# A two-layer decoder trunk on one core: other first loads, a first step by k tiles, and the first three blocks of each layer in turn by pairs of k tiles

## The chip, the cores and the metric

The kernel runs on one core of one Trainium2 chip. The metric is the device time of one execution in microseconds, as the median of three runs. Engines are called by the names of the profile: PE is TensorE, DVE VectorE, ACT ScalarE, POOL GpSimd and SP SyncE (which here only issues transfers).

## What is computed

The reference is a decoder trunk of two layers, for one sequence of 256 tokens with 2048 channels, all in float32:

```python
proj = rms_norm(x, norm_g) @ w_in        # 2048 -> D_IN columns, cut into segments
mixed = [fox(q, k, v, f), diff(q, k, v), moba(q, k, v), gla(q, k, v, a)]   # each 512 wide
gated = concat([group * silu(gate) for group, gate in zip(mixed, gates)])
x = x + gated @ w_out                    # 2048 -> 2048
```

and, after the second layer, one more RMS norm. This is the reference in outline: FoX is attention with a forget gate, diff the difference of two softmax maps, MoBA attention over chosen blocks of keys, and GLA a linear attention whose gate comes from a narrow projection `gla_a` (16 columns) through a matrix `gla_wa2` and a log-sigmoid.

## The kernel before

**Products.** A float32 product is made of three products of rounded parts: each weight `raw` is split into `hi` (a rounded copy, made by ACT, `hi_of`, line 425) and `lo = raw - hi` (DVE, `lo_of`, line 428). The left side, the normalised and transposed input, lies in SBUF as `hTp` with a high and a low half for each of its 16 k tiles of 128 channels. PE then multiplies high by hi, low by hi, and high by lo (`multiply`, line 1169; the matmul itself is issued by a helper on line 276).

**Steps.** The weights stream through in steps (`_steps`, line 133). A block is a range of up to 512 output columns, and a step is two k tiles of a block. A step costs one transfer into `raw` (four buffers), one hi, one lo (four buffers each) and 12 matmuls: 3 products, 2 k tiles, 2 halves of 128 tokens. `prepare(i)` makes hi and lo of step i and issues the load of step i + 4; it is called three steps ahead of `multiply`. All these loads go through SP's queue, in the order of the program.

**The first three blocks of a layer.** Block 0 has 348 columns (`gla_a` and a part of a gate), block 1 has 512 (GLA's q and k), block 2 has 348 (a gate's rest, FoX's forget gate, a part of FoX's v). Their 24 steps are interleaved, by the sort key on line 140: before, two steps of block 0, two of block 1, two of block 2, and so on. Blocks 0 and 1 accumulate in the PSUM pool `mm` (two buffers), block 2 in a `side` buffer. All other blocks follow one by one. Steps are counted from 0, so that step 24 is the first behind the three blocks.

**The start.** PE first runs `WARM` matmuls on zeros (line 368). The first loads are: x^T, in chunks of four k tiles (`load_x`, line 1086; the first chunk in two halves), the norm's weights `ngt`, the first step's weights in two halves (the first half on ACT's queue, the second on SP's), the next three steps' weights, and a table of constants `ct` on ACT's queue (line 1234). x^T is scaled and split into `hTp` by `split_xt`, k tiles 0 and 1 on DVE, the others' high half on ACT.

**What hangs on the first blocks.** Once the last step of a block is multiplied, `settle` evicts it. From block 0 comes `an` (the 16 gate columns), which PE transposes with `ct`'s identity; DVE copies it to `at`; PE makes `al` from `at` and `wa`; ACT and DVE make its log-sigmoid (`two`, with two loads of a function table) and DVE its running sum. From block 1 come GLA's q and k (`four`): DVE transposes them in squares, SP writes them to DRAM in four transfers `far<-four` (line 310), POOL reads them back turned (`four<-far`, line 312), and ACT puts them in order (`four<-four`, 128x1024). From block 2 come `fx`, FoX's forget gate, with a log-sigmoid of its own (`fe`), and `ct,fh` and `ct,fl` products of FoX's chain. All GLA pieces meet in the factors `eight` and `tq` and in the product `side<-tq,eight` on PE, which stands behind step 40 in layer 0 and behind step 184 in layer 1. These pieces are background tasks, written as generators: `tick` (line 257) runs some of their pieces after each step, into the same in-order queues in which hi, lo, loads and matmuls stand. So what the program writes first, an engine does first.

**At the layer's end** `residual` adds the out-projection to `xs` on DVE (`xs<-mm,xs`) and so frees an `mm` buffer for the next layer's blocks.

Of the kernel before, what the change touches and what calls it, by code (L numbers as in the profile page):

```python
# [21 lines left out]
P = 128  # L22
SEQ = 256
# [10 lines left out]
NEG = -1.0e30  # L34
RAW_BUFS = 4
PART_BUFS = 4
WARM = 10
X_AT = (24, 28, 32, 36)
T4 = 10
T2 = 6  # L40
# [88 lines left out]
LAYER = 20  # L129
FIRST = tuple(l * LAYER + i for l in range(DEPTH) for i in range(3))  # L130


def _steps():


    steps = []
    for i, b in enumerate(_BLOCKS):
        per = b["per"]
        for j in range(0, KT, per):
            key = (i // LAYER * LAYER, j // 4, i) if i in FIRST else (i, 0, i)  # L140
            if b["w"] == "w_out" and b["cols"][0][0] < 1024:
                key = (i - b["cols"][0][0] // 512, max(j // 4, 1), i)
            steps.append((key, len(steps), {"block": i, "kts": b["kts"][j:j + per], "first": j == 0, "last": j + per == KT}))
    steps = [s for _, _, s in sorted(steps, key=lambda z: z[:2])]
    at = 0
    for s in steps:
        s["at"] = at
        at += P * len(s["kts"]) * _BLOCKS[s["block"]]["n"]
    return steps


def in_steps(w_in, w_out):

    w, flat = {"w_in": w_in, "w_out": w_out}, []
    for s in _steps():
        b = _BLOCKS[s["block"]]
        for_kt = [np.concatenate([w[b["w"]][b["l"], k * P:(k + 1) * P, c:c + n] for c, n in b["cols"]], 1) for k in s["kts"]]
        flat.append(np.stack(for_kt, 1).reshape(-1))
    return np.concatenate(flat)
# [48 lines left out]
def hybrid_trunk(  # L208
# [17 lines left out]
    nc = tc.nc  # L226
# [14 lines left out]
    s4 = Slots(wk, "four", T4)  # L241
# [32 lines left out]
    def matmul(out, lhsT, rhs, start, stop, tiles=1):  # L274
        left["pe"] += int(np.prod(rhs.shape[1:])) * (4 if lhsT.dtype == F32 else 1) / 2400.0 / tiles
        t_.matmul(out, lhsT, rhs, start=start, stop=stop)  # L276
# [57 lines left out]
    ct = cp.tile([P, CONST["f"].shape[1]], F32, name="ct")  # L334
    ngt = cp.tile([P, DEPTH, KT], F32, name="ngt")
# [29 lines left out]
    def keep_warm(n):  # L365
        warm = side.get([P, 1024])
        for _ in range(n):
            t_.matmul(warm[:, :512], zeros[:, :P], zeros, start=True, stop=True)
        side.put(warm)

    keep_warm(WARM)
    nc.scalar.activation(halfpow, halfpow, AF.Copy)
# [52 lines left out]
    def hi_of(hi, src, scale=1.0):  # L425
        a_.activation(hi, src, AF.Copy, scale=scale)

    def lo_of(lo, src, hi):
        v_.tensor_sub(lo, src, hi.bitcast(F32))
# [649 lines left out]
    plan = []  # L1079
    for z in _steps():  # L1080
        b = blocks[z["block"]]
        plan.append({**z, "block": b, "need": {(b["need"], b["l"], k // 4) for k in z["kts"]}})

    xts = []

    def load_x(chunk):
        xts.append(s4.get([P, 4, SEQ]))
        if chunk == 0:
            nc.sync.dma_start(ngt, norm_gt)
        for part in (slice(0, 2), slice(2, 4)) if chunk == 0 else (slice(0, 4),):  # L1090
            nc.sync.dma_start(xts[chunk][:, part], xt[:, chunk * 4 + part.start:chunk * 4 + part.stop])

    def load(i):
        s = plan[i]
        if i < 24 and i % 6 == 0:
            load_x(i // 6)
        per, n = s["block"]["per"], s["block"]["n"]
        raw = wst.tile([P, STEP_W], F32, name="raw", bufs=RAW_BUFS)
        raw = raw[:, :per * n]
        s["raw"] = raw.rearrange("p (j c) -> p j c", j=per)  # L1100
        src = weights[s["at"]:s["at"] + P * per * n].rearrange("(p c) -> p c", p=P)
        if i == 0:
            nc.scalar.dma_start(raw[:, :n], src[:, :n])
            nc.sync.dma_start(raw[:, n:], src[:, n:])
        else:
            nc.sync.dma_start(raw, src)

    def xt_hi(kt):
        src, g = xts[kt // 4][:, kt % 4], ngt[:, 0, kt:kt + 1]
        if kt < 2:  # L1110
            v_.tensor_scalar(hT[0][:, kt], src, g, None, op0=OP.mult)
        else:
            hi_of(hT[0][:, kt], src, g)

    def xt_lo(kt):
        v_.scalar_tensor_tensor(hT[1][:, kt], xts[kt // 4][:, kt % 4], ngt[:, 0, kt:kt + 1], hT[0][:, kt].bitcast(F32),
                                op0=OP.mult, op1=OP.subtract)

    def split_xt(kts):

        for kt in kts:
            xt_hi(kt)
        for kt in kts:
            xt_lo(kt)
        if kts[-1] % 4 == 3:
            ready.add(("h", 0, kts[-1] // 4))
# [29 lines left out]
    def parts_of(s):  # L1156
        per, n = s["block"]["per"], s["block"]["n"]
        for name in ("hi", "lo"):
            if s["block"]["kind"] == "apart":
                s[name] = s4.get([P, per, n], F32R)  # L1160
                continue
            t = wst.tile([P, PART_W], F32R, name=name, bufs=PART_BUFS)
            s[name] = t[:, :per * n].rearrange("p (j c) -> p j c", j=per)
        if s is plan[0] or s is plan[1]:
            split_xt(s["kts"])
        hi_of(s["hi"], s["raw"])
        lo_of(s["lo"], s["raw"], s["hi"])

    def multiply(s):
        b = s["block"]  # L1170
        n, (lh, ll) = b["n"], b["lhs"]
        if s["first"]:
            b["ps"] = side.get([P, 1024]) if b["aside"] else mm.tile([P, 1024], F32, name="mm")
        ps = b["ps"]
        if b["kind"] == "apart":
            b.setdefault("steps", []).append(s)
            if s["last"]:
                b["ps1"] = side.get([P, 1024])
            for m, o, steps in ((0, ps[:, :n], [s]), (1, b.get("ps1"), b["steps"])):
                if m == 1 and not s["last"]:  # L1180
                    break
                for z in steps:
                    for j, kt in enumerate(z["kts"]):
                        first, last = z["first"] and j == 0, z["last"] and j == len(z["kts"]) - 1
                        hi, lo, ts = z["hi"][:, j], z["lo"][:, j], slice(m * P, (m + 1) * P)
                        matmul(o[:, :n], lh[:, kt, ts], hi, first, False)
                        matmul(o[:, :n], lh[:, kt, ts], lo, False, False)
                        matmul(o[:, :n], ll[:, kt, ts], hi, False, last)
            return
        order = list(enumerate(s["kts"]))  # L1190
        end = s["last"], len(order) - 1
        for x, part in ((lh, "hi"), (ll, "hi"), (lh, "lo")):
            for j, kt in order:
                for m in range(2):
                    matmul(ps[:, m * 512:m * 512 + n], x[:, kt, m * P:(m + 1) * P], s[part][:, j],
                           s["first"] and j == 0 and x is lh and part == "hi", part == "lo" and (True, j) == end)
# [12 lines left out]
    ahead = PART_BUFS - 1  # L1209

    def prepare(i):
        if 0 < i < 24 and i % 6 == 0:
            split_xt([i // 6 * 4 + k for k in range(4)])
        if i < len(plan):
            parts_of(plan[i])
        if i + RAW_BUFS < len(plan):
            load(i + RAW_BUFS)
# [13 lines left out]

    for i in range(RAW_BUFS):
        load(i)
    nc.scalar.dma_start(ct, const)
    for i in range(ahead):
        prepare(i)
    s4.put(zeros)
    g_.memset(tq, 0.0)
    tasks += [constants()]
# [2 lines left out]
    for i, s in enumerate(plan):  # L1242
        if ("r", 0) not in ready:
            next(rms, None)
        prepare(i + ahead)
        if i in X_AT:
            c = slice(X_AT.index(i) * 512, X_AT.index(i) * 512 + 512)
            nc.sync.dma_start(xs[:, :, c], x[0, :, c].rearrange("(m p) c -> p m c", p=P))
        settle(waiting, s["first"] and len(waiting) > 1)
        while not s["need"] <= ready:  # L1250
            tick(False)
        multiply(s)
        if s["last"] and s["block"]["done"]:
            waiting.append(s["block"])
        give_time()
        tick()
    while tasks:
        tick(False)
    b = plan[-1]["block"]
# [31 lines left out]
```

## Time and profile before

| | us |
|---|---|
| median of three runs (lowest, highest) | 919.61 (918.66, 920.67) |
| the profiled execution | 920.54 |
| its span in the trace | 918.8 |
| PE busy in it | 901.3 |
| DVE busy | 571.5 |
| ACT busy | 524.6 |
| first real matmul | 7.70 |
| GLA's product in layer 0, layer 1 | 111.43, 560.76 |

All times in the profile are from the start of the span, and 1.7 us of the execution lie outside it. A row of the timeline gives start, length, engine, line, operation and tiles, the number of instructions run together, and in brackets how long the engine stood idle before it and what released it. Lines are those of the kernel; L178 is where a helper records all operations of DVE and ACT, so those are told apart by their tiles. PE's matmuls are pipelined, and its busy time includes the time at a lower granted clock.

### The profile page before, as it was taken

What the parts mean: (1) busy time and instruction counts of PE and PEld (TensorE: products, weight loads), DVE (VectorE), ACT (ScalarE), POOL (GpSimd) and SP (SyncE); (2) the same over time, 40 slices, a digit from 0 to 9 for tenths busy, and PEclk for the clock granted to TensorE, in tenths of its full rate; (3) what the DMA queues carried; (4) which work ended last, traced back from release to release, by engine and by line L of the source; (5) the groups of instructions that cost most, each with busy time, mean ns of one, the idle gap of its engine ahead of it and who ended that gap; (6) DMA issues with size and microseconds to landing.
All of it is one profiled execution on the core that took longest, in us unless ns stands there. A gap on an engine that the chain in (4) does not pass through costs nothing.

```text
span 918.8 us, 12421 instructions
## 1 busy us (share of the span) xinstructions
PE 901.3 (98%) x4490; PEld 766.8 (83%) x4490; DVE 571.5 (62%) x831; ACT 524.6 (57%) x819; POOL 38.6 (4%) x55
## 2 busy tenths in 40 slices
PE   8999999999999999999999999999999999999996
PEld 6988789888888888888899887988888888878886
DVE  6765887566558556555655568856655674565662
ACT  6588654664455556535565784566444654754441
POOL 0000000000000010000000000010000000110000
PEclk9999999999999999999999999999999999999998
DMA  8767656587656947757776466667877687587652
GB/s 264 255 206 263 234 182 240 167 301 263 233 183 205 319 156 236 276 200 259 235 231 212 145 235 194 192 212 213 290 231 228 172 264 274 159 307 254 193 164 92
DMA packets 77455, 205.34 MB, mean 223 GB/s; under 512 B 9265, under 2 KB 29137, under 8 KB 77394
## 3 DMA queue, kind: packets, MB, share of 16 engines
q1 hardware_dynamic: 70496, 183.44, 60.7%
q0 software_dynamic: 5408, 19.40, 6.1%
q10 hardware_dynamic: 1490, 1.71, 0.6%
q8 instruction: 35, 0.57, 0.2%
q14 instruction: 26, 0.21, 0.1%
HBM read 184.07 MB, written 20.45 MB: 223 GB/s over the span
## 4 chain that ended last, share of the span: by engine, by line
PE 86%; DMA 4%; ACT 3%; DVE 2%; issue 2%; SPq 1%; DVEq 0%; POOLq 0%; POOL 0%; ACTq 0%
PE mm L276 77%; PE side L276 9%; DMA four<-far 3%; DMA far<-four 1%; ACT hi L178 1%; ACT four L178 1%; DVE lo L178 1%; SPq L310 1%; DMA raw<-in_weights 1%; ACT L178 0%; DVE four L178 0%; DVE tq L178 0%; DVE eight L178 0%; ACT two L178 0%; DVE two L178 0%
## 5 line engine op out<-in xcount | busy, mean ns | idle before, releaser
L178 DVE TENSOR_TENSOR lo<-raw,hi 128x1024 fp32r<-128x1024 f32 (+1 forms) x316 | 368.4, 1170 | 305.4 <-ACT hi L178 288.5
L178 ACT ACTIVATE hi<-raw 128x1024 fp32r<-128x1024 f32 (+1 forms) x316 | 319.1, 1017 | 301.6 <-PE mm L276 244.1
L276 PE MATMUL mm<-hi,hTp 128*128 128x512 f32 (+1 forms) x1920 | 461.3, 382 | 2.6 <-ACT hi L178 2.6
L276 PEld LDWEIGHTS mm<-hi,hTp 128*128 128x128 f32 x1920 | 352.3, 188 | 68.1 <-ACT hi L178 3.9
L276 PE MATMUL mm<-lo,hTp 128*128 128x512 f32 (+1 forms) x960 | 248.3, 380 | 0.0
L276 PEld LDWEIGHTS mm<-lo,hTp 128*128 128x128 f32 x960 | 177.8, 188 | 32.7
L276 PE MATMUL mm<-hi,mTh 128*128 128x512 f32 (+1 forms) x256 | 64.6, 377 | 0.0
L276 PE MATMUL mm<-hi,mTl 128*128 128x512 f32 (+1 forms) x256 | 64.4, 376 | 0.0
L276 PE MATMUL mm<-lo,mTh 128*128 128x512 f32 (+1 forms) x256 | 64.4, 376 | 0.0
L276 PEld LDWEIGHTS mm<-lo,mTh 128*128 128x128 f32 x256 | 46.2, 188 | 8.8
L276 PEld LDWEIGHTS mm<-hi,mTl 128*128 128x128 f32 x256 | 46.2, 188 | 8.7
L276 PEld LDWEIGHTS mm<-hi,mTh 128*128 128x128 f32 x256 | 46.1, 188 | 8.7
L312 POOL DMA_DIRECT2D four<-far x32 | 17.2, 538 | 617.2 <-DMA far<-four 266.3
L276 PE MATMUL side<-four,four 128*128 128x128 f32 (+1 forms) x320 | 37.3, 277 | 1.9 <-DMA four<-far 1.9
L276 PEld LDWEIGHTS side<-four,four 128*128 128x128 f32 (+1 forms) x320 | 34.1, 190 | 4.6 <-DMA four<-far 2.5
L178 DVE STREAM_TRANSPOSE four<-four 128x1024 f32<-128x1024 f32 x24 | 29.5, 1230 | 0.0
L178 ACT ACT_TABLE_LOAD x22 | 28.2, 1283 | 0.3
L178 ACT ACTIVATE four<-mm,rstd 128x512 f32<-128x512 f32 (+1 forms) x40 | 24.4, 661 | 0.1
L276 PE MATMUL side<-hi,hTp 128*128 128x348 f32 x128 | 22.9, 321 | 0.0
L178 ACT ACTIVATE four<-side 32x64 f32<-32x64 f32 (+2 forms) x28 | 8.8, 342 | 24.3 <-PE side L276 24.3
L276 PEld LDWEIGHTS side<-hi,hTp 128*128 128x128 f32 x128 | 20.8, 188 | 1.3 <-issue 0.7
L178 ACT ACTIVATE four<-side,nb 128x256 f32<-128x256 f32 (+1 forms) x48 | 20.4, 437 | 1.5 <-DVE nb L178 1.2
(135 smaller groups left out, 500.1 us busy)
## 6 DMA issues: line engine op xcount, KB each, us to landing
raw<-in_weights SPq DMA_DIRECT2D x272, 512.0 KB, 4.3
far<-four SPq DMA_DIRECT2D x128, 128.0 KB, 4.2
four<-far POOLq DMA_DIRECT2D x32, 512.0 KB, 6.4
raw<-in_weights SPq DMA_DIRECT2D x47, 348.0 KB, 3.4
xs<-in_x SPq DMA_DIRECT2D x4, 512.0 KB, 5.1
four<-in_xt SPq DMA_DIRECT2D x3, 512.0 KB, 5.6
far<-two SPq DMA_DIRECT2D x24, 64.0 KB, 3.6
two<-far POOLq DMA_DIRECT2D x6, 256.0 KB, 5.2
```

The lines of the kernel that those rows point to most:

```text
L178: return f(*args, **kw)
L276: t_.matmul(out, lhsT, rhs, start=start, stop=stop)
L310: nc.sync.dma_start(d[:, :, i].rearrange("j c f -> c j f"), t[32 * i:32 * i + 32].rearrange("c (j f) -> c j f", j=4))
L312: g_.dma_start(t, d.rearrange("j c i f -> (j c) (i f)"))
```

## The change

It has four parts.

- **First loads.** SP's queue begins with the first half of the first weights, then `ngt`, the second half, the second step's weights, x^T's k tiles 2 and 3, then the next steps. ACT's queue begins with x^T's k tiles 0 and 1; the constants `ct` are issued there only after the first three `prepare`. `load_x` is written for any range of k tiles.
- **First step.** hi, lo and the matmuls of step 0 are done k tile by k tile, and x^T is split into `hTp` by two k tiles every third step, no longer by four every sixth.
- **Order.** The key of the first three blocks goes from `j // 4` to `j // 2`, in both layers: one step of block 0, one of block 1, one of block 2, and so on.
- **Warm-up.** `WARM` goes from 10 to 9.

```diff
-WARM = 10
+WARM = 9
...
-            key = (i // LAYER * LAYER, j // 4, i) if i in FIRST else (i, 0, i)
+            key = (i // LAYER * LAYER, j // 2, i) if i in FIRST else (i, 0, i)
...
-    def load_x(chunk):
-        xts.append(s4.get([P, 4, SEQ]))
-        if chunk == 0:
-            nc.sync.dma_start(ngt, norm_gt)
-        for part in (slice(0, 2), slice(2, 4)) if chunk == 0 else (slice(0, 4),):
-            nc.sync.dma_start(xts[chunk][:, part], xt[:, chunk * 4 + part.start:chunk * 4 + part.stop])
+    def load_x(eng, a, b):
+        if a % 4 == 0:
+            xts.append(s4.get([P, 4, SEQ]))
+        eng.dma_start(xts[a // 4][:, a % 4:(b - 1) % 4 + 1], xt[:, a:b])
...
-        if i < 24 and i % 6 == 0:
-            load_x(i // 6)
+        if 0 < i < 24 and i % 6 == 0:
+            load_x(nc.sync, i // 6 * 4, i // 6 * 4 + 4)
...
         if i == 0:
-            nc.scalar.dma_start(raw[:, :n], src[:, :n])
+            nc.sync.dma_start(raw[:, :n], src[:, :n])
+            load_x(nc.scalar, 0, 2)
+            nc.sync.dma_start(ngt, norm_gt)
             nc.sync.dma_start(raw[:, n:], src[:, n:])
         else:
             nc.sync.dma_start(raw, src)
+        if i == 1:
+            load_x(nc.sync, 2, 4)
...
-        if s is plan[0] or s is plan[1]:
+        if s is plan[0]:
             split_xt(s["kts"])
+            for j in range(2):
+                hi_of(s["hi"][:, j], s["raw"][:, j])
+                lo_of(s["lo"][:, j], s["raw"][:, j], s["hi"][:, j])
+            return
...
-        for x, part in ((lh, "hi"), (ll, "hi"), (lh, "lo")):
-            for j, kt in order:
+        products = [(x, part, j, kt) for x, part in ((lh, "hi"), (ll, "hi"), (lh, "lo")) for j, kt in order]
+        if s is plan[0]:
+            products.sort(key=lambda z: z[2])
+        for x, part, j, kt in products:
...
-        if 0 < i < 24 and i % 6 == 0:
-            split_xt([i // 6 * 4 + k for k in range(4)])
+        if 0 < i < 24 and i % 3 == 0:
+            split_xt((i // 3 * 2, i // 3 * 2 + 1))
...
-    nc.scalar.dma_start(ct, const)
     for i in range(ahead):
         prepare(i)
+    nc.scalar.dma_start(ct, const)
```

On PE, right behind the warm matmuls, there stands before:

```order
L276 MATMUL mm<-hi,hTp 128x348 x8
L276 MATMUL mm<-lo,hTp 128x348 x4
L276 MATMUL mm<-hi,hTp 128x348 x8
L276 MATMUL mm<-lo,hTp 128x348 x4
L276 MATMUL mm<-hi,hTp 128x512 x8
L276 MATMUL mm<-lo,hTp 128x512 x4
```

and now (`side_205` is block 2's buffer):

```order
L276 MATMUL mm<-hi,hTp 128x348 x4
L276 MATMUL mm<-lo,hTp 128x348 x2
L276 MATMUL mm<-hi,hTp 128x348 x4
L276 MATMUL mm<-lo,hTp 128x348 x2
L276 MATMUL mm<-hi,hTp 128x512 x8
L276 MATMUL mm<-lo,hTp 128x512 x4
L276 MATMUL side_205<-hi,hTp 128x348 x8
L276 MATMUL side_205<-lo,hTp 128x348 x4
```

Step 0 is cut in two by k tiles, and the second step is one of block 1, the third one of block 2.

At the end of layer 0's first three blocks PE had, with `al` as `side_658`, behind step 22 of block 2:

```order
L280 MATMUL side_610<-ct,an 16x128 x2
L276 MATMUL mm<-hi,hTp 128x512 x8
L276 MATMUL mm<-lo,hTp 128x512 x4
L276 MATMUL side_250<-hi,hTp 128x348 x8
L276 MATMUL side_250<-lo,hTp 128x348 x4
L276 MATMUL side_658<-at_91,wa 128x256 x2
L276 MATMUL side_250<-hi,hTp 128x348 x8
L276 MATMUL side_250<-lo,hTp 128x348 x4
L276 MATMUL mm<-hi,hTp 128x512 x8
L276 MATMUL mm<-lo,hTp 128x512 x4
```

and now, with `al` as `side_701`:

```order
L280 MATMUL side_642<-ct,an 16x128 x2
L276 MATMUL side_205<-hi,hTp 128x348 x8
L276 MATMUL side_205<-lo,hTp 128x348 x4
L276 MATMUL mm<-hi,hTp 128x512 x8
L276 MATMUL mm<-lo,hTp 128x512 x4
L276 MATMUL side_701<-at_91,wa 128x256 x2
L276 MATMUL mm<-hi,hTp 128x512 x8
L276 MATMUL mm<-lo,hTp 128x512 x4
```

The transposes of `an` go from behind step 20 to behind step 22, `al` from behind step 22 to behind step 24.

On SP in layer 0, at the far transfers of GLA's q and k, there stands before:

```order
L1106 DMA raw<-in_weights 128x1024 x8
L1248 DMA xs<-in_x 128x2x512
L1106 DMA raw<-in_weights 128x1024
L310 DMA far_743<-four_718 32x4x256 x4
L1106 DMA raw<-in_weights 128x1024 x3
L1248 DMA xs<-in_x 128x2x512
```

and now:

```order
L1106 DMA raw<-in_weights 128x1024 x8
L1256 DMA xs<-in_x 128x2x512
L1106 DMA raw<-in_weights 128x1024 x2
L310 DMA far_763<-four_736 32x4x256 x4
L1106 DMA raw<-in_weights 128x1024 x2
L1256 DMA xs<-in_x 128x2x512
```

The four far transfers stand behind one weight load more; in layer 1 it is the same, without the loads of x. On ACT the two log-sigmoids, `two` and `fe`, stand together now, with block 2's evictions ahead of them, and a layer has one load of a function table less.

## Prediction

> **What bounds the kernel now.** I read the page first: span, busy shares, and the chain's shares by engine.
>
> ```profile
> span 918.8 us, 12421 instructions
> PE 901.3 (98%) x4490; PEld 766.8 (83%) x4490; DVE 571.5 (62%) x831; ACT 524.6 (57%) x819; POOL 38.6 (4%) x55
> PE 86%; DMA 4%; ACT 3%; DVE 2%; issue 2%; SPq 1%; DVEq 0%; POOLq 0%; POOL 0%; ACTq 0%
> ```
>
> TensorE is busy for 901.3 of 918.8 us: 17.5 us of gaps is all that an edit of order can win, unless it also moves TensorE's clock. The waits of TensorE (line, what it waited for: sum, times, longest):
>
> ```profile
> PE side L276 <- DVE eight L178: 3.0, 2, 1.7
> PE mm L276 <- ACT hi L178: 2.6, 2, 2.1
> PE side L276 <- DMA four<-far: 1.9, 3, 1.0
> PE side L368 <- DVE halfpow L362: 1.2, 1, 1.2
> ```
>
> Two of these rows lie where the change works: the wait for `hi` has 2.1 us in one piece, at the start; the two waits for `eight` are GLA's, one for each layer. Next the start, as the timeline has it (start, length, engine, work, idle time ahead and its releaser):
>
> ```profile
> 1.19 4.45 PE L368 MATMUL side<-four 128*128 128x512 bf16 x10 [1.19 <-DVE halfpow L362]
> 4.94 0.62 DVE L178 TENSOR_SCALAR hTp<-four,ngt 128x256 fp32r<-128x256 f32 x2 [3.52 <-DMA four<-in_xt]
> 5.47 0.88 DVE L178 SCALAR_TENSOR_TENSOR hTp<-four,ngt,hTp 128x256 fp32r<-128x256 f32 x2
> 6.86 0.78 ACT L178 ACTIVATE hi<-raw 128x696 fp32r<-128x696 f32 x1 [4.62 <-DMA raw<-in_weights]
> 7.68 0.88 DVE L178 TENSOR_TENSOR lo<-raw,hi 128x696 fp32r<-128x696 f32 x1 [1.33 <-ACT hi L178]
> 7.70 1.59 PE L276 MATMUL mm<-hi,hTp 128*128 128x348 f32 x8 [2.06 <-ACT hi L178]
> 9.68 1.06 ACT L178 ACTIVATE hi<-raw 128x1024 fp32r<-128x1024 f32 x1 [0.50 <-DMA raw<-in_weights]
> 13.14 1.09 PE L276 MATMUL mm<-hi,hTp 128*128 128x512 f32 x4
> ```
>
> The warm matmuls end at 5.64, real work starts at 7.70, because the second half of the first weights lands last (ACT waits for `raw` until 6.86); x^T was there at 4.94. The two 348-wide steps are done at 13.14. The same stretch by windows, and one window around GLA's wait of layer 1 (after the engines come the granted clock, the DMA share and GB/s):
>
> ```profile
> 5.70:9.00 3.30, 1.30 (x8) 1.30 (x9) 1.97 (x5) 2.14 (x4) 0.00 (x0) 1.00 1.03 387
> 9.00:10.20 1.20, 1.20 (x6) 1.20 (x5) 1.15 (x2) 0.70 (x2) 0.00 (x0) 0.51 1.01 282
> 10.20:12.50 2.30, 2.30 (x9) 2.30 (x9) 1.23 (x1) 2.30 (x3) 0.00 (x0) 0.51 0.83 247
> 550.00:565.00 15.00, 13.30 (x66) 10.95 (x66) 12.76 (x31) 9.07 (x14) 0.00 (x0) 1.00 0.59 196
> ```
>
> After a stretch in which TensorE was busy for 1.30 of 3.30 us, the clock stands at 0.51 from 9.0 to 12.5. So the late start costs its gap and some 1.7 us of half speed. A gap of 1.70 us in a busy stretch (layer 1's GLA wait) leaves it at 1.00.
>
> **The first loads.** What a step should take is seen in the chain (six steps of the first three blocks in two rows):
>
> ```profile
> 22.53 9.23 PE mm L276 x48
> 31.76 3.77 PE side L276 x24
> ```
>
> 24 matmuls of 348 columns take 3.77 us, a step of 12 thus 1.88; the other row is two such steps and two of 512, so one of 512 takes (9.23 − 3.77)/2 = 2.73. At full pace two 348-wide steps need 3.77 us, and they took 13.14 − 7.70 = 5.44: the half clock's part is 1.67.
>
> After the change the DMA engines carry the same kinds of bytes, in another order. When the pieces came:
>
> ```profile
> four<-in_xt SPq DMA_DIRECT2D x2, 256.0 KB, 4.2
> raw<-in_weights ACTq DMA_DIRECT2D x1, 174.0 KB, 3.5
> ```
>
> The first half of the weights, issued at 1.2 on ACT's queue, took 3.5 us; it now heads SP's. x^T's first two k tiles take its old place on ACT's, beside the same 174 + 16 + 256 KB as before, so I leave them at 4.94; with the constants' 289 KB gone from ahead of the weights, the second half and block 1's first step come earlier. By hand: nine warm matmuls of 0.445 us end at 5.2; DVE has the first k tile's hT at 4.94 + 0.31 = 5.25, so the first matmul starts near 5.3 (was 7.70). On DVE follow the rest of hT (0.62 + 0.88 in all, to 6.4) and two lo of half width (0.44 each, half of 0.88), to 7.3; the last six matmuls (0.94) behind them end at about 8.1. ACT's two half-width hi (0.4 each) need the second weight half by about 6.5, which the 6.86 of before, less 289 KB, allows. Block 1's hi and lo (1.06, then about 1.3) want their 512 KB by about 7; 1132 KB stand in the queues up to them, and before the change about as much (1165 KB, counted by issues: ngt, two of x^T, both halves, constants) was in by 6.86. So no wait follows. To compare like with like I add one 348-wide step: 8.1 + 1.88 = 9.98 against 13.14, **−3.16 us**. Ends: x^T a microsecond later gives −2.2; no gap at all would give −3.6.
>
> Nothing shows that real matmuls at 5.3 run at full pace. The ten warm ones took 0.445 us each with 512 columns, the 512-wide ones at 13.14 take 1.09/4 = 0.27: the array is slow at first, and the first real ones met it awake at 7.70 (1.59/8 = 0.20 each). Bounds: nothing, or all of step 0 at half pace (+1.88, where the waits for DVE don't hide it, as they do for about 0.9). I take +0.3, near nothing, since by 5.3 the array has been busy for four microseconds. [...]
>
> **The order by pairs.** TensorE's work is the same, but the blocks 0, 1, 2 now end one step apart and at the end of their 24 steps. Everything that hangs on them (an's transposes, the gate product `al`, its log-sigmoid) moves two steps later in the program, while GLA's product stays behind step 40 (layer 0) and step 184 (layer 1). Layer 1's rows, from `al`'s log-sigmoid to the product:
>
> ```profile
> 509.90 0.60 ACT L178 ACTIVATE two<-side 128x512 f32<-128x512 f32 x1 [0.62 <-PE side L276]
> 514.30 1.04 ACT L178 ACTIVATE hi<-raw 128x1024 fp32r<-128x1024 f32 x1
> 514.53 1.75 PE L276 MATMUL mm<-hi,hTp 128*128 128x512 f32 x7
> 520.85 1.39 SPq L310 DMA_DIRECT2D far<-four  x3
> 521.87 0.21 ACT L178 ACTIVATE fe<-fx 128x8 f32<-128x8 f32 x1 [2.69 <-DVE fx L178]
> 525.03 2.00 ACT L178 ACTIVATE hi<-raw 128x1024 fp32r<-128x1024 f32 x2
> 526.12 2.11 PE L276 MATMUL mm<-hi,hTp 128*128 128x512 f32 x8 [0.55 <-ACT hi L178]
> 526.42 0.53 POOL L312 DMA_DIRECT2D four<-far  x1 [53.30 <-ACT hi L178]
> DMA to landing us min/median/max: 4.0/4.0/4.0
> 535.29 1.05 ACT L178 ACTIVATE four<-four 128x1024 f32<-128x1024 f32 x1
> 560.76 1.80 PE L276 MATMUL side<-tq,eight 128*128 128x128 f32 x14 [1.70 <-DVE eight L178]
> ```
>
> ACT holds the log-sigmoid for 514.30 − 509.90 = 4.40 us and fox's (`fe`) for 525.03 − 521.87 = 3.16. Now `al` comes with the end of step 24, and both stand together on ACT ahead of the next hi: 514.53 + 4.40 + 3.16 = 522.1, hi 1.0, a lo of 1024 columns 0.88 × 1024/696 = 1.3, to 524.4. SP has one more weight load ahead of the far DMAs (the order shows it) and that load waits for this lo: far at about 524.85, 4.0 later than 520.85, that is 10.3 after step 25's start. In exchange ACT has one table load less and one hi fewer between put-in-order and the product: 560.76 − 535.29 = 25.47 becomes about 24.5. TensorE gets to the product 560.76 − 1.70 − 0.55 − 514.53 = 43.98 after step 25's start. So the data must have returned by 43.98 − 24.5 = 19.5, and from the far issue there are 19.5 − 10.3 = **9.2 us**. The round trip was 526.42 + 4.0 − 520.85 = 9.57 here. In layer 0:
>
> ```profile
> 71.53 0.43 SPq L310 DMA_DIRECT2D far<-four  x1
> 78.46 0.70 POOL L312 DMA_DIRECT2D four<-far  x1 [27.25 <-DVE f L178]
> DMA to landing us min/median/max: 6.5/6.5/6.5
> 111.43 1.80 PE L276 MATMUL side<-tq,eight 128*128 128x128 f32 x14 [1.28 <-DVE eight L178]
> ```
>
> 78.46 + 6.5 − 71.53 = 13.4. There a load of x stood just ahead in SP's queue; now one more weight load lies between.
>
> Layer 0: stall = round trip − 9.2 in place of 1.28. Ends: 9.57 gives 0.4 (−0.9), 13.4 gives 4.2 (+2.9). I take 10.8, nearer to layer 1's since the load of x is out of the way: 1.6, **+0.35**. Layer 1: before, 1.70 + 0.55 = 2.25 of stalls; 0.55 (for hi behind `fe`) goes, since `fe` moves ahead. Round trip 10.2 (9.57 and some way behind one more load): 1.0; ends 9.57 and 13.4 as above (−1.9 and +2.0). At the layer's boundary block 1 now takes the second place, and with it the mm buffer that the residual frees:
>
> ```profile
> 459.85 1.28 DVE L178 TENSOR_TENSOR xs<-mm,xs 128x512 f32<-128x512 f32 x2
> 460.20 1.41 PE L276 MATMUL mm<-hi,hTp 128*128 128x348 f32 x8
> ```
>
> The residual reads it to 461.13, or, with a hi and a lo of 696 columns ahead in the place of 1024 (0.28 and about 0.4 shorter), about 460.5: TensorE waits 0.3 to 0.4, once (I take 0.37). Layer 1: 1.0 + 0.37 − 2.25 = **−0.88**.
>
> At nothing: the later constants (first wanted some twenty steps on), the split of x^T by pairs (same instructions), step 0's halves on ACT and DVE (two fixed costs more, counted above), the raw ring (unchanged depth).
>
> **The sum.** Against the profiled execution, 920.54 us (span 918.8): −3.16 + 0.3 + 0.35 − 0.88 = −3.4, **917.1**. That execution lies 0.93 above the median of 919.61. I leave 917.1 as it stands: the sum takes the half clock's 1.67 out, and an execution of before that had no half clock would have begun lower and won less, to the same end.
>
> **The rivals.** *B, slower: GLA's rows come back late.* The product's chain has no slack left, and each microsecond of round trip beyond 9.2 stalls TensorE. With 13.4 in both layers: 4.2 − 1.28 + 4.2 + 0.37 − 2.25 = +5.2, less 2.86: 922.9; with a half-clock stretch behind such a gap (as 1.7 at the start) 924.6. It decides from 921.45 on, where the two round trips sum to 25.4. For it: layer 0's 13.4. Against: layer 1's 9.57, without x's load. 0.15.
> *C: the first real matmuls are slow.* The clock is not yet up at 5.3, or a stretch at half clock follows step 0's waits: step 0 at half pace, or one such stretch of 1.7, less the 0.3 already counted, +1.3 to +1.6: 918.4 to 918.7. For it: the warm matmuls' 0.445 against 0.27; TensorE works only 1.9 of the 2.9 us that step 0 takes. Against: the gap of 1.70 at 559 that left 1.00. 0.2. [...]
> *D: the first bytes come no earlier.* The windows show DMA at 1.03 of its share from 5.7 to 9.0. If x^T shares the engines with 174 + 512 KB of weights issued at once, it lands at about 6 and block 1 at 8.5, and the start wins 1.5 in place of 2.9: 918.5. [...] 0.1.
> *E: the chains fit.* Round trips under 9.3: layers −1.28 and −1.9: 914.5 to 915.5. 0.13.
>
> **How the numbers follow.** The forecast has 0.42 (own range 915.8 to 917.7). 0.2% is 1.84 us, about what a measurement of this kernel can tell from no change: faster is under 917.77, slower over 921.45. Faster: forecast and E, 0.55. Same: C and D, 0.30. Slower: B, 0.15. The range, 914.6 to 921.8, takes in C and D, nearly all of E and the milder half of B, and leaves out B's worse half and the tail under E.
>
> **What would show it.** Right: the first real matmul at 5.2 to 5.6, no granted clock of 0.51 before 13 us, the third step's start by 11; far DMAs of GLA about 10 us after step 25's start; waits for `eight` of 0.4 to 2 in both layers; a wait of 0.3 at 460. Wrong: an x^T landing after 6; slow matmuls after 5.3; waits for `eight` over 3, or none; a new wait that I don't name.

## The result and the profile after

The changed kernel takes 925.77 us (median of six runs, 923.73 to 928.62), against 919.61 for the kernel before; the ratio is 1.0067, with a 95% interval of 1.0048 to 1.0085. It is slower by 0.7%, outside the range of the prediction. The profiled execution took 925.39 us. In two of the experiments one slow execution (1524.1 us in the order alone, 3708.2 us in the changed kernel once more) stands in the median that is given, but not in the ratio.

The head of the page: the span is 4.8 us longer, and TensorE is busy for 2.7 us more with the same matmuls.

```profile
span 923.6 us, 12419 instructions
PE 904.0 (98%) x4489; PEld 767.0 (83%) x4489; DVE 571.1 (62%) x832; ACT 522.9 (57%) x818; POOL 38.3 (4%) x55
```

TensorE's waits, after (line, what it waited for: sum, times, longest):

```profile
PE mm L276 <- ACT hi L178: 5.8, 3, 2.4
PE side L276 <- DMA four<-far: 2.1, 2, 1.5
PE side L276 <- DVE eight L178: 1.9, 2, 1.0
PE side L368 <- DVE halfpow L362: 1.2, 1, 1.2
PE mm L276 <- DVE xs L178: 0.4, 1, 0.4
```

The waits for `eight` fell, as I had forecast (to 2.6 in all), from 3.0 to 1.9. But the wait for `hi` went from 2.6 to 5.8, in three pieces: one at the start, and one that was not there before in each layer. The start, after, on the timeline:

```profile
5.01 1.15 PE L276 MATMUL mm<-hi,hTp 128*128 128x348 f32 x4
6.40 0.58 PE L276 MATMUL mm<-lo,hTp 128*128 128x348 f32 x2 [0.24 <-DVE lo L178]
7.45 0.47 PE L276 MATMUL mm<-lo,hTp 128*128 128x348 f32 x2
7.89 1.06 ACT L178 ACTIVATE hi<-raw 128x1024 fp32r<-128x1024 f32 x1 [1.37 <-DMA raw<-in_weights]
9.00 2.12 PE L276 MATMUL mm<-hi,hTp 128*128 128x512 f32 x8 [1.08 <-ACT hi L178]
13.75 0.48 PE L276 MATMUL mm<-hi,hTp 128*128 128x348 f32 x2
```

Real work starts at 5.01 in place of 7.70, and no half clock follows (the granted clock is 1.00 from 9.0 to 13.0, where it was 0.50 from 9.03 to 12.44 before). The fourth step, with two of 348 and one of 512 columns done, begins at 13.75; before, the same work was done at 13.14 + 2.73 = 15.87. The start thus wins 2.1 us, in spite of a new gap of 1.08 us for block 1's weights.

By layer 0's GLA product the 2.1 us are gone and 2.1 more are lost (113.50 against 111.43). These rows of SP, POOL, ACT and PE show how:

```profile
64.41 2.12 PE L276 MATMUL mm<-hi,hTp 128*128 128x512 f32 x8
74.70 2.18 SPq L310 DMA_DIRECT2D far<-four  x4
80.15 0.70 POOL L312 DMA_DIRECT2D four<-far  x1 [24.47 <-DMA far<-four]
DMA to landing us min/median/max: 8.8/8.8/8.8
88.98 1.06 ACT L178 ACTIVATE four<-four 128x1024 f32<-128x1024 f32 x1 [5.08 <-DMA four<-far]
95.91 3.89 ACT L178 ACTIVATE hi<-raw 128x1024 fp32r<-128x1024 f32 x4
97.01 3.61 PE L276 MATMUL mm<-hi,hTp 128*128 128x512 f32 x8 [2.38 <-ACT hi L178]
113.50 1.80 PE L276 MATMUL side<-tq,eight 128*128 128x128 f32 x14 [0.97 <-DVE eight L178]
```

Step 25 starts at 64.41. SP issues the far transfers at 74.70, 10.29 later. The data is back at 88.95, after a round trip of 14.25 us. ACT's put-in-order waits 5.08 us for it. The hi of the next steps stand behind it on ACT, the first at 89.95, and those from 95.91 on also behind an eviction and a scaling that it held up too; TensorE runs out of them and stands for 2.38 us. Then its eight 512-wide matmuls take 3.61 us, not 1.98, since the granted clock has fallen (0.50 from 97.24 to 100.65); the windows show it (granted clock, DMA share and GB/s at the end):

```profile
90.00:97.00 7.00, 4.63 (x21) 3.51 (x19) 2.51 (x9) 5.57 (x14) 0.00 (x0) 1.00 0.43 156
97.00:99.00 2.00, 1.99 (x5) 1.59 (x6) 2.00 (x2) 2.00 (x3) 0.00 (x0) 0.56 0.00 0
```

Layer 1 is the same again: far at 527.68, 10.34 behind step 25's 517.34; data back after 14.2 us.

```profile
533.44 0.53 POOL L312 DMA_DIRECT2D four<-far  x1 [54.31 <-DMA far<-four]
541.83 1.06 ACT L178 ACTIVATE four<-four 128x1024 f32<-128x1024 f32 x1 [4.94 <-DMA four<-far]
549.86 2.66 PE L276 MATMUL mm<-hi,hTp 128*128 128x512 f32 x8 [2.30 <-ACT hi L178]
566.35 1.80 PE L276 MATMUL side<-tq,eight 128*128 128x128 f32 x14 [0.95 <-DVE eight L178]
```

At the layer's boundary there is the wait of 0.43 us for the buffer that the residual frees; 0.37 were forecast.

### The profile page after: what moved, and what is told of

It reads as the page before. It is cut to its first block, busy times and chain, and to the rows that moved or that the text cites. A ratio compares the mean times of both kernels' runs of the same rounds, so it can differ in the third digit from the quotient of the medians.

```text
span 923.6 us, 12419 instructions
## 1 busy us (share of the span) xinstructions
PE 904.0 (98%) x4489; PEld 767.0 (83%) x4489; DVE 571.1 (62%) x832; ACT 522.9 (57%) x818; POOL 38.3 (4%) x55
## 5 line engine op out<-in xcount | busy, mean ns | idle before, releaser
L178 DVE TENSOR_TENSOR lo<-raw,hi 128x1024 fp32r<-128x1024 f32 (+2 forms) x317 | 368.6, 1167 | 311.5 <-ACT hi L178 288.1
L178 ACT ACTIVATE hi<-raw 128x1024 fp32r<-128x1024 f32 (+2 forms) x317 | 319.2, 1014 | 308.5 <-PE mm L276 243.3
L178 ACT ACTIVATE four<-mm,rstd 128x512 f32<-128x512 f32 (+1 forms) x40 | 24.5, 664 | 0.1
L178 ACT ACTIVATE four<-four 128x1024 f32<-128x1024 f32 x14 | 14.8, 1056 | 14.2 <-DMA four<-far 12.3
```

The costliest lines, as they stand in the source:

```text
L178: return f(*args, **kw)
```

## The experiments

The theory after the result, A: the order by pairs puts both log-sigmoids ahead of a hi, its lo frees the weight buffer that SP waits for, and behind that load on SP stand the far transfers; the loss is all in this chain. The rivals: B, that the new first loads shift the stream so that it collides; C, that the return is slow whenever it starts; D, that the loss is only the place of put-in-order ahead of hi on ACT. Each group of four runs was timed with the kernel before on the same chip, where that took 921.3 to 921.4 us; so the ratios count.

**New loads, old order.** The change without its order:

```diff
-            key = (i // LAYER * LAYER, j // 2, i) if i in FIRST else (i, 0, i)
+            key = (i // LAYER * LAYER, j // 4, i) if i in FIRST else (i, 0, i)
...
             nc.sync.dma_start(raw[:, n:], src[:, n:])
+            load_x(nc.sync, 2, 4)
         else:
             nc.sync.dma_start(raw, src)
-        if i == 1:
-            load_x(nc.sync, 2, 4)
...
+        if s is plan[1]:
+            split_xt(s["kts"])
...
-        if 0 < i < 24 and i % 3 == 0:
-            split_xt((i // 3 * 2, i // 3 * 2 + 1))
+        if 0 < i < 24 and i % 6 == 0:
+            split_xt([i // 6 * 4 + k for k in range(4)])
```

> The new first loads, the split first step and nine warm matmuls, with the order of before (key j // 4; x^T's k tiles 2 and 3 are loaded ahead of step 1's weights, which needs them). Theory A, that all the loss comes from the order by pairs through GLA's way out and back: GLA's far transfers come about 5 to 6.5 us after step 25's start as before, no wait for hi near step 36 or step 180, the waits for eight stay 1.3 and 1.7; only the start's gain is left, 1 to 2.5 us: 917 to 918.5 us. Theory B, that the loss comes from the whole stream of weight loads standing at another place after the new start, so that the return collides with it: the waits for hi behind put-in-order come here too, 921 us or more.

Measured: 918.04 us, ratio 0.9972 (0.9954 to 0.9989). TensorE's waits for `eight` in the two layers are those of before (the first row is the start):

```profile
8.82 1.52 PE L276 MATMUL mm<-hi,hTp 128*128 128x348 f32 x8 [0.77 <-ACT hi L178]
109.11 1.80 PE L276 MATMUL side<-tq,eight 128*128 128x128 f32 x14 [1.29 <-DVE eight L178]
558.64 1.80 PE L276 MATMUL side<-tq,eight 128*128 128x128 f32 x14 [1.67 <-DVE eight L178]
```

1.29 and 1.67 against 1.28 and 1.70, and no wait for hi behind put-in-order. B falls: the new loads alone win, by 0.3%. In layer 0 the return of q and k took 3.8 us here, against 6.5 before the change, and the wait for `eight` is the same: in the old order it did not hang on the return.

**The order alone**, on the loads of before:

```diff
-            key = (i // LAYER * LAYER, j // 4, i) if i in FIRST else (i, 0, i)
+            key = (i // LAYER * LAYER, j // 2, i) if i in FIRST else (i, 0, i)
...
-        if 0 < i < 24 and i % 6 == 0:
-            split_xt([i // 6 * 4 + k for k in range(4)])
+        if 0 < i < 24 and i % 3 == 0:
+            split_xt((i // 3 * 2, i // 3 * 2 + 1))
```

> The order by pairs in both layers with the loads, the whole first step and the ten warm matmuls of before. Theory A: the two losses behind layer 0's and layer 1's first blocks are here as in the changed kernel, 2.3 us of waiting for hi, 0.7 to 1.6 us of half clock and about 1 us for eight in each layer, and the start wins nothing: 926 to 928 us, slower than the changed kernel by 1 to 2. Theory B: without the new start the returns land in 10 us or less and the kernel stands within 1.5 us of 919.6.

Measured: 926.39 us, ratio 1.0056 (1.003 to 1.0081). The order alone brings the loss:

```profile
98.12 2.11 PE L276 MATMUL mm<-hi,hTp 128*128 128x512 f32 x8 [1.44 <-ACT hi L178]
114.62 1.80 PE L276 MATMUL side<-tq,eight 128*128 128x128 f32 x14 [2.60 <-DVE eight L178]
565.52 1.80 PE L276 MATMUL side<-tq,eight 128*128 128x128 f32 x14 [2.56 <-DVE eight L178]
```

The sum of the waits is as large as expected in layer 0 (4.0 us), but in this execution more of it stands at `eight`, and layer 1 has no wait for hi at all; its 2.56 us are less than expected. The interval is too wide to tell from this run whether the new start is worth its 2.1 us.

**The far transfers one load earlier.** The changed kernel, with one `yield` moved for GLA's q and k (`now` is true for these alone):

```diff
-        yield
+        if not now:
+            yield
         d = yield from far.take([4, 32, 4, x * 32])
...
         yield
+        if now:
+            yield
         g_.dma_start(t, d.rearrange("j c i f -> (j c) (i f)"))
```

> The changed kernel, with the four far transfers of GLA's q and k issued one weight load earlier on SP in both layers, right behind the transposes; everything else stands at the same place (POOL's read back and put-in-order too). Theory A, that the far transfers wait on SP behind a weight load whose buffer the two log-sigmoids hold: far is issued about 4 to 5 us after step 25's start in place of 10.3, put-in-order finds its data, the waits for hi (2.4 and 2.3 us), their half clock and most of the waits for eight go: 917 to 918.5 us. Theory C, that the return is slow because it shares the DMA engines with the weight loads that are set free together, whenever it starts: put-in-order still waits 1 to 3 us and the time is 920 to 923 us.

Measured: 915.88 us, ratio 0.9937 (0.9916 to 0.9959), the fastest of all. Layer 0's rows:

```profile
64.75 2.12 PE L276 MATMUL mm<-hi,hTp 128*128 128x512 f32 x8
68.94 2.16 SPq L311 DMA_DIRECT2D far<-four  x4
73.86 0.70 POOL L315 DMA_DIRECT2D four<-far  x1 [17.78 <-DMA far<-four]
DMA to landing us min/median/max: 3.8/3.8/3.8
84.20 1.04 ACT L178 ACTIVATE four<-four 128x1024 f32<-128x1024 f32 x1
108.70 1.80 PE L276 MATMUL side<-tq,eight 128*128 128x128 f32 x14
```

Far leaves 4.2 us after step 25's start in place of 10.3, put-in-order finds its data, and TensorE waits for nothing there; in layer 1 0.16 us for `eight` is left. So the loss hung on one place in SP's queue (A). The return landed in 3.8 us, so it is not slow by itself (C falls). The time is 1.1 us below A's range: the waits that the kernel before had, 1.28 and 1.70 for `eight` and 0.55 for hi, are all but gone too.

**Put-in-order two steps later.**

```diff
         w, v = yield from turned(s4, squares(t), lambda: s4.put(t))
+        yield
+        yield
         env["gla_qk", l] = yield from put_in_order(s4, w, v)
```

> The changed kernel, with put-in-order of GLA's q and k two steps later on ACT and its product one step later on PE; far transfers and read back as in the changed kernel. Theory A: far is still issued 10.3 us after step 25's start and returns 14 us later; the hi no longer stand behind the wait, so the 2.4 and 2.3 us and the half clock go, but the chain behind put-in-order is as late as before less one step, so 1 to 2.5 us of waiting for eight remain in each layer: 919 to 921.5 us. Theory D, that put-in-order's place ahead of hi on ACT is the whole loss: waits for eight under 0.5 us, 916 to 917.5 us.

Measured: 916.72 us, ratio 0.9952 (0.9934 to 0.9971): D's number, not A's. The far transfers were as late as in the changed kernel, and their data was back after 13.2 us, at 87.7; still TensorE does not wait for this product:

```profile
74.54 1.90 SPq L310 DMA_DIRECT2D far<-four  x4
89.27 1.05 ACT L178 ACTIVATE four<-four 128x1024 f32<-128x1024 f32 x1
110.59 1.72 PE L276 MATMUL side<-tq,eight 128*128 128x128 f32 x14
```

My number for A left something out. Put to product is now 110.59 − 89.27 = 21.3 us and not 24.5, since two hi and an eviction have gone ahead of put-in-order, and the product stands one step (2.7) later. Together the chain may be 5.9 us later, which is more than the 4 us that it was late. So the run does not part A from D; it shows that a later deadline mends nearly as much as an earlier start. A wait of 0.92 and 0.93 us for `eight` now stands in the two layers at a later product (at 143.15 and 590.85). What speaks against D is layer 1 of the order alone: there nothing waited for hi, and TensorE still stood for 2.56 us.

**The loads of x later**, in the changed kernel:

```diff
-X_AT = (24, 28, 32, 36)
+X_AT = (48, 52, 56, 60)
```

> The changed kernel with the four loads of x moved from steps 24, 28, 32, 36 to 48, 52, 56, 60, so that none runs beside layer 0's return of q and k; layer 1 has no such load and is the control. Theory C', that the return takes 8.8 us because other transfers run beside it: layer 0's return falls to 7 us or less, the wait for hi behind put-in-order from 2.4 to at most 1, and the time by 1 to 3 us; layer 1 keeps its 8.4 us and 2.3 us. Theory F, that a return issued that late takes 8 to 9 us for another reason: layer 0's stays at 8 us or more and the time within 0.5 us of the changed kernel.

**The changed kernel once more**, without an edit, in the same group:

> The changed kernel itself on the chip of this group, to compare the others with: 925 to 928 us, 2.2 to 2.5 us of waiting for hi behind put-in-order in each layer; which of the two layers shows half clock behind it, and how long, may differ.

Measured: 924.42 us with the loads of x later, ratio 1.0032 (1.0017 to 1.0047), and 925.22 us for the changed kernel, 1.0045 (1.003 to 1.0061). The changed kernel's waits for hi were only 0.91 and 1.92 this time, and those for `eight` 2.59 in both layers, so that the split of the loss varies from run to run. Its sum does not much: with 1.7 us for each stretch at half clock (two in the changed kernel, one here, behind layer 1's wait, where the product takes 3.07 us against 1.80 in layer 0) it is 10.0 us in the changed kernel and 9.7 here. Its rows in layer 0:

```profile
74.49 1.87 SPq L310 DMA_DIRECT2D far<-four  x4
87.30 1.06 ACT L178 ACTIVATE four<-four 128x1024 f32<-128x1024 f32 x1 [3.61 <-DMA four<-far]
95.34 2.12 PE L276 MATMUL mm<-hi,hTp 128*128 128x512 f32 x8 [0.91 <-ACT hi L178]
```

The returns (transfer, us to landing; MB of weights and x that the same engines moved meanwhile, by windows from issue to landing) stand beside each other so:

| | return, us | other MB |
|---|---|---|
| far ahead, layer 0 | 3.8 | 0.29 |
| before, layer 1 | 4.0 | 0.36 |
| loads of x later, layer 0 | 5.5 | 1.16 |
| before, layer 0 | 6.5 | 1.42 |
| changed again, layer 0 | 7.2 | 1.94 |
| changed, layer 1 | 8.4 | 1.78 |
| changed, layer 0 | 8.8 | 2.63 |

A longer return leaves more time for other bytes, so the table alone shows no cause; but per microsecond, too, the two short returns had 0.08 and 0.09 MB beside them and the others 0.21 to 0.30. Moving x out of the way took layer 0's return from 7.2 to 5.5 us and its waits from 3.5 to 1.9. The control, layer 1, had 7.2 against 8.0 us, so about half of the difference in the return might be chance. The two medians differ by 0.8 us with overlapping intervals: the direction is C' (that other transfers beside the return make it long), the size in the time stays open.

**The order 0, 2, 1 within a pair**, on the kernel with far ahead:

```diff
-            key = (i // LAYER * LAYER, j // 2, i) if i in FIRST else (i, 0, i)
+            key = (i // LAYER * LAYER, j // 2, (0, 2, 1)[i % LAYER]) if i in FIRST else (i, 0, i)
```

> The kernel with far transfers one load earlier, and within each pair the 348-wide block 2 second and the 512-wide block 1 third, in both layers. If the start's remaining wait of 0.8 to 1.4 us is for the 512 KB of block 1's first step, it falls to 0.5 or less, and the boundary's 0.44 us goes, since block 2 needs no mm buffer; block 1's q and k come one step (2.7 us) later, so the far transfers too, by up to 3 to 5 us. Theory A (each microsecond that far comes later than about 5 behind step 25 shows behind put-in-order once the slack is used): put-in-order waits 0 to 2 us and the two nearly cancel: 914 to 917 us. If the far transfers' time does not matter: 914 to 915 and no wait at put-in-order.

Measured: 917.28 us, ratio 0.9962 (0.9946 to 0.9978), just above both ranges. The start's wait fell to 0.23 us and the boundary's went, as expected. Put-in-order did not wait; the program had moved the GLA tasks a step later, product included. In place of the gains stand waits of 0.66 and 0.71 us for `an`, whose block now ends just ahead of its transposes, and 0.92 and 1.09 for a later product. So this order is not better, through waits that I had not named.

**Step 0 whole**, on the kernel with far ahead:

```diff
-            for j in range(2):
-                hi_of(s["hi"][:, j], s["raw"][:, j])
-                lo_of(s["lo"][:, j], s["raw"][:, j], s["hi"][:, j])
-            return
...
-        if s is plan[0]:
-            products.sort(key=lambda z: z[2])
```

> The kernel with far transfers one load earlier, but with step 0's hi, lo and matmuls whole, as before the change. If the split of step 0 carries part of the start's gain: the first real matmul waits for both halves of the weights, at about 6.5 in place of 5.1, step 1 then begins when its own hi is there, at 8.9 to 9.4 as with the split, since that wait of 0.8 to 1.3 us covers it: no change of time, within 0.5 us of the kernel with the split, but a gap of more than 1 us ahead of step 0 that may bring a stretch of half clock (plus 1.0 to 1.7). If the split matters: 1 us or more without a half clock.

Measured: 916.71 us, ratio 0.9949 (0.993 to 0.9968), 0.8 us above the kernel with the split; the intervals overlap, so whether the split is worth anything in time stays open. The profile shows what the split guards against:

```profile
6.62 2.69 PE L276 MATMUL mm<-hi,hTp 128*128 128x348 f32 x8 [1.41 <-ACT hi L178]
10.13 2.01 PE L276 MATMUL mm<-hi,hTp 128*128 128x512 f32 x8
```

Real work starts at 6.62, behind a gap of 1.41 us, and its first eight matmuls take 2.69 us, against 1.59 for the same eight before the change. This is the slow first step of the prediction's third rival, though in this experiment and not in the changed kernel.

## Why the prediction was wrong

**The start (−3.16, less 0.3): right in kind, 0.7 too large.** The first matmul came at 5.01 (5.3 forecast) and step 0 ended at 7.92 (8.1), its second half at full pace (0.79 us for four matmuls, as at 13.12; the first four took 1.15). What failed is "no wait follows": block 1's first weights landed at 7.9 and not by 7. The rate was not the reason: from 1.0 to 6.86 us the DMA engines moved 1.38 MB, before the change 1.42. But the 1132 KB (1.16 MB) that I had counted up to these weights were in only when 1.77 MB had been moved, so loads issued behind them had moved beside them. The start measured −2.1.

**Far at 10.3 behind step 25: right.** 10.29 and 10.34.

**The slack of 9.2 us: right.** "Stall = round trip − 9.2" can be held against six layers in which no half clock falls between put-in-order and the product (round trip from the far issue to put-in-order's start; stall as the sum of the waits for hi and `eight`):

| | round trip | less 9.2 | measured |
|---|---|---|---|
| changed again, layer 0 | 12.8 | 3.6 | 0.91 + 2.59 = 3.5 |
| changed again, layer 1 | 13.8 | 4.6 | 1.92 + 2.59 = 4.5 |
| order alone, layer 0 | 13.3 | 4.1 | 1.44 + 2.60 = 4.0 |
| order alone, layer 1 | 11.9 | 2.7 | 2.6 |
| x later, layer 0 | 11.0 | 1.8 | 1.9 |
| x later, layer 1 | 13.0 | 3.8 | 1.15 + 2.60 = 3.8 |

**The round trips (10.8 and 10.2): here it failed.** They were 14.25 and 14.2. I took them from layer 1's 9.57 and gave only some way for one more load ahead. But I had worked out in the same paragraph that the far transfers wait for a lo that comes late; the same lo and its followers set the weight loads free that had stood still. In layer 0 SP issued none from 67.1 to 74.3 us, then four at 74.3, 77.0, 78.8 and 80.9, with one of x at 79.2, and these ran beside the return. That this traffic made it long was tested only for the loads of x, where the direction came out and the size stayed open. The 4.0 us that I read for layer 1's return belonged to a quiet stretch (0.36 MB beside it), as the 3.8 us of the kernel with far ahead do. The 13.4 of layer 0, which I put down to the load of x, was the better guide. With the measured sizes my own sum gives 920.54 − 2.1 + (5.05 − 1.28) + (4.96 + 0.43 − 2.25) = 925.35, and the profiled execution took 925.39. That it fits to 0.04 is luck: the last store was issued 5.7 us later than before (918.70 against 913.02), 0.9 more than the sum has, and the span ended 4.9 us behind it in place of 5.8. (In the recorded sum, layer 0's 1.6 − 1.28 is 0.32 and not 0.35, which changes nothing.)

**Where the stall stands** I had not seen: part of it comes as a wait for hi, since hi stand behind put-in-order on ACT. In the changed kernel's layer 0 it is 2.38 for hi, 1.71 of half clock (3.41 us at half pace) and 0.97 for `eight`, 5.06 together, against 14.25 − 9.2 = 5.05; in layer 1 it is 2.30 + 1.71 + 0.95 = 4.96, against 4.96. While the chain is late, TensorE can as well be slow as stand still, so the half clock cost nothing more there. By this split my sign of being right, waits for `eight` of 0.4 to 2, came true by luck while the stall was 5 us in each layer.

**The boundary: right** (0.43 against 0.37). **The rivals:** B, with its place, was the case; its price of 922.9 was short by 1.6 for the round trips (13.4 in place of 14.25 and 14.2) and by 0.8 for the start. I gave it 0.15; with layer 0's row as good as layer 1's it should have had about half. C and E were not the case; D's wait for block 1 was there, 1.08 us long.

## What to carry to other kernels

A transfer's time read in one place of a trace holds for the traffic of that place (3.8 to 8.8 us here for the same 512 KB): when an edit moves a transfer, look at what else is set free at its new time, loads that wait for the same buffers above all. A transfer that must go out early should not stand in a queue behind a load whose buffer a late chain frees: on SP the load stood until 74.3 and the far transfers followed at 74.70, and this one place was worth 1% here (ratios to the kernel before of 1.0045 and 0.9937). And a reorder should be followed to every deadline that it does not move: the product stayed behind step 40 while its inputs moved two steps.

## What the runs showed of the hardware that was not expected

The return of GLA's q and k, 512 KB in one and the same form, took 3.8 to 8.8 us; the table puts it beside what ran meanwhile.

Half clock followed a gap only sometimes. In the traces of the kernel before and of the changed one, each stretch at half clock between two pieces of work lasted 3.41 us: 9.03 to 12.44 before, 97.24 to 100.65 and 551.21 to 554.62 in the changed kernel (read from the granted clock in windows of 0.1 us). It began 1.33, 0.23 and 1.35 us after TensorE had gone back to work, and in the 3.41 us up to its start TensorE had been busy for 0.40, 0.30 and 0.40 of the time. In the changed kernel the two starts lie 453.97 us apart, 133 times 3.4133; before, the starts at 9.03 and at 913.56, behind the last matmuls, lie 904.53 us apart, 265 times 3.4133. The gaps, and what came behind them (GLA's product takes 1.80 us at a granted clock of 1.00):

| gap | behind it |
|---|---|
| before, start, 2.06 us | granted clock 0.50 |
| changed, layer 0, 2.38 us | granted clock 0.50 |
| changed, layer 1, 2.30 us | granted clock 0.50 |
| changed again, layer 1, 2.59 us | GLA's product in 3.07 us |
| changed again, layer 0, 2.59 us | GLA's product in 1.80 us |
| order alone, layer 0, 2.60 us | granted clock 1.00 |
| before, layer 1, 1.70 us | granted clock 1.00 |

So the length of a gap alone did not tell whether half clock followed: 2.06 us was followed by it, 2.60 us in the order alone cost only itself, and 2.59 us in one and the same execution came out both ways. What decides it is not shown by these runs.

With step 0 whole the first twelve matmuls took from 6.62 to 10.13, 3.51 us, against 1.88 for such a step at full pace, although TensorE had worked from 1.2 to 5.2. The granted clock reads 1.00 there, as it does for the warm matmuls of 0.45 us each, so this goes by their lengths. Ahead of them lay the gap of 1.41 us; in the changed kernel, with real work from 5.01 on and no gap over 0.24 us in step 0, the second half of that step ran at full pace.
